# The end of a layer norm rearranged: tile 7's bias transfer ahead of tile 2's squares, tile 2 finished by VectorE in halves, one operation for the mean, epsilon on GpSimd

## The chip, the cores and the metric

One core of a Trainium2 chip runs the whole kernel. The metric is the device time in microseconds (us) of one execution; the kernel before has a median of 386.59 us over three runs (385.78 to 387.56). Engines are named as the profile names them: PE (TensorE), DVE (VectorE), ACT (ScalarE), POOL (GpSimd), SP (SyncE, which here only issues transfers).

## The reference

One decoder layer on 1024 tokens of width 1024: an input projection, three branches (spatial gating, a state-space scan, cross-attention), an output projection, and a post-norm. The change touches only the last line of it:

```
y = concatenate([y_a * silu(g_a), y_b * silu(g_b), y_x * silu(g_x)], axis=-1)
x = layer_norm(DN_ALPHA * x + y @ w_out[layer], ln_g[layer], ln_b[layer])
# layer_norm: mu = mean(x); xc = x - mu; var = mean(xc*xc)
#             xc * rsqrt(var + 1e-5) * g + b
```

## The kernel before

Tokens lie in eight tiles of 128 rows; `res[:, t]` (128x1024) holds tile t. The output projection is done in Strassen fashion, as seven products of 512-column blocks (p1 to p7), each matrix product in three passes over split operands (lines 144 to 146). The last stretch (lines 1193 to 1237) computes the last blocks tile by tile in the order of tiles 4, 5, 0, 6, 1, 7, 2, 3, and normalises a tile as soon as its last block has been added. PE, DVE, ACT and POOL execute in the order in which the code is written (`ordered("a")`, line 1043); SP's order is the scheduler's, and follows when data become ready.

For a tile t but 3 the steps are:

- `first` and `more` (DVE, lines 1094 and 1101) add a PSUM bank to `res`, and leave row sums.
- `means` (lines 1059 to 1067): two small DVE operations make minus the mean; then ACT squares the centred tile and sums it (`junk`, line 1066).
- `deviations` (1069 to 1072): DVE scales the sum and adds epsilon, POOL raises it to the power -0.5.
- `centre` (1075): DVE subtracts the mean and multiplies by gamma, in place. It therefore has to wait until ACT's squares of the same tile are done.
- `finish` (1078 to 1089): for tiles 4, 5, 6, 7 and 2 ACT multiplies by the inverse deviation (1082), a transfer issued by POOL adds the bias `lnb2` (1083), and a transfer to DRAM follows when that has landed (1084, on SP; for tile 2 on ACT's queue). For tiles 0, 1 and 3 DVE does scale and bias in one operation (1087), and the transfer goes out on SP (1089).

Tile 3 comes last. Its mean and variance come from `bn_stats` of three pieces and `bn_aggr` (1227 to 1233), epsilon is added on DVE (1234), the power is POOL's (1235), the centring DVE's (1236), and `finish(3, (0, 480, 832, 1024))` writes it out in three pieces.

Of the kernel before, what the change touches and what calls it, by code (L numbers as in the profile page):

```python
# [36 lines left out]
def trunk_kernel(ctx, tc, xT, x, w_gq, w_kv, memT, w_fm, w_v, w_o,  # L37
                 gm_wT, gm_bs, gm_g, gm_lnb, sp, b1, b2, c1, c2, dsk, glu_w, glu_b,
                 ln_gb, out):
    nc = tc.nc  # L40
# [1007 lines left out]
    stat = gm.tile([P, 64], F32, tag="nv", name="stat")  # L1048


    sums = stat[:, 0:16].rearrange("p (t c) -> p t c", c=2)
    nmean, ssq, rsd = stat[:, 16:24], stat[:, 24:32], stat[:, 32:40]
    bst = stat[:, 40:58].rearrange("p (c s) -> p c s", s=6)
    bmv = stat[:, 58:60]

    def at(t):
        return t - 4 if t >= 4 else t + 4

    def means(t0, n):
        i = slice(at(t0), at(t0) + n)  # L1060
        V.tensor_tensor(nmean[:, i], sums[:, i, 0], sums[:, i, 1], op=ALU.add)
        V.tensor_scalar(nmean[:, i], nmean[:, i], -1.0 / 1024, None, op0=ALU.mult)  # L1062
        for t in range(t0, t0 + n):
            junk = gm.tile([P, 1024], BF16, tag="mt", bufs=2, name=f"junk{t}")
            i1 = slice(at(t), at(t) + 1)
            S.activation(junk, res[:, t], AF.Square, bias=nmean[:, i1], scale=1.0,  # L1066
                         accum_out=ssq[:, i1])

    def deviations(t0, n):
        i = slice(at(t0), at(t0) + n)  # L1070
        V.tensor_scalar(rsd[:, i], ssq[:, i], 1.0 / 1024, LN_EPS, op0=ALU.mult, op1=ALU.add)  # L1071
# [2 lines left out]
    def centre(t):
        V.scalar_tensor_tensor(res[:, t], res[:, t], nmean[:, at(t):at(t) + 1], lng,
                               op0=ALU.add, op1=ALU.mult)

    def finish(t, cuts=None, queue=nc.sync):
# [237 lines left out]
```

## Time and profile before

| | us |
|---|---|
| median of three runs | 386.59 |
| the profiled execution, its own time | 383.81 |
| its span, first to last instruction | 382.1 |
| PE busy | 367.4 (96%) |
| DVE busy | 293.8 (77%) |
| ACT busy | 181.5 (48%) |
| POOL busy | 96.7 (25%) |

The span leaves 1.7 us of the profiled execution outside it. All times below are counted from the span's start. Busy shares are means over the whole program; the change lies in the last 40 us, where the profile is read instruction by instruction. A row of the timeline gives start, duration, engine, line, operation, what is written and read, and in brackets how long the engine stood idle before and what released it.

### The profile page before, as it was taken

To read this page: it belongs to the slowest core of one execution; us is meant where nothing else is said; L and a number is where in the kernel's file an instruction comes from. 1 tells how busy PE (TensorE), PEld (TensorE's weight loads), DVE (VectorE), ACT (ScalarE), POOL (GpSimd) and SP (SyncE) were. 2 spreads that over 40 slices of the span, in tenths; PEclk is the share of its full clock that TensorE was granted. 3 is DMA by queue.
4 is the path that set the end of the run, shared out by engine and by line. 5 is a ranking of instruction groups with operands and counts; after the bars stand their busy time and mean duration, and the time that the engine had idled before them with its cause. 6 is when DMAs were issued, how large, how long until landed. Compare 5 with 4: busy or idle time off the path is not lost.

```text
span 382.1 us, 5532 instructions
## 1 busy us (share of the span) xinstructions
PE 367.4 (96%) x1877; PEld 310.0 (81%) x1877; DVE 293.8 (77%) x639; ACT 181.5 (48%) x349; POOL 96.7 (25%) x87
## 2 busy tenths in 40 slices
PE   8999999999999999999999999999999999999980
PEld 7888898888888788888888888888888888877870
DVE  4699897988886599969788459775538997777783
ACT  4573597567774635232132334333424667545430
POOL 1305000001000593860873800500000022003541
PEclk9999999999999999999999999999999999999995
DMA  7984436237899776202212232400107959820988
GB/s 221 302 274 124 131 112 192 86 98 206 171 188 235 189 196 162 60 29 58 69 41 60 55 95 62 165 2 0 57 4 214 380 152 225 208 84 0 256 224 235
DMA packets 28628, 53.69 MB, mean 141 GB/s; under 512 B 5928, under 2 KB 9400, under 8 KB 27448
## 3 DMA queue, kind: packets, MB, share of 16 engines
q1 hardware_dynamic: 26296, 44.43, 38.0%
q0 software_dynamic: 2160, 8.39, 11.8%
q10 hardware_dynamic: 144, 0.52, 0.4%
q8 instruction: 15, 0.25, 0.3%
q14 instruction: 13, 0.11, 0.1%
HBM read 44.87 MB, written 13.63 MB: 153 GB/s over the span
## 4 chain that ended last, share of the span: by engine, by line
PE 67%; DVE 19%; issue 4%; ACT 4%; DMA 3%; POOL 1%; SPq 0%; POOLq 0%; DVEq 0%; ACTq 0%
PE zg L151 4%; PE zg L152 4%; PE zg L154 4%; PE zv L144 3%; PE zv L146 3%; PE zv L145 3%; PE av L624 2%; PE zxb L152 2%; PE zxb L154 2%; PE zxb L151 2%; PE q L152 2%; PE q L154 2%; PE q L151 2%; DVE l_u L62 2%; DMA r_wo<-in_w_o_dram 2%
## 5 line engine op out<-in xcount | busy, mean ns | idle before, releaser
L144 PE MATMUL zv<-h_v,xh 128*128 128x512 f32 x64 | 25.6, 400 | 0.3 <-ACT yb L229 0.3
L151 PE MATMUL zu<-xh,h_u 128*128 128x512 f32 x64 | 25.9, 404 | 0.0
L151 PE MATMUL zg<-xh,h_g 128*128 128x512 f32 x64 | 25.5, 398 | 0.0
L152 PE MATMUL zu<-xl,h_u 128*128 128x512 f32 x64 | 25.0, 391 | 0.0
L152 PE MATMUL zg<-xl,h_g 128*128 128x512 f32 x64 | 25.0, 390 | 0.0
L146 PE MATMUL zv<-h_v,xl 128*128 128x512 f32 x64 | 25.0, 390 | 0.0
L145 PE MATMUL zv<-l_v,xh 128*128 128x512 f32 x64 | 24.9, 389 | 0.0
L1029 POOL DMA_DIRECT2D l_wo<-ws_s x6 | 5.2, 863 | 72.8 <-ACT l_wo L1028 66.0
L65 ACT CAST h_v<-r_v 128x512 fp32r<-128x512 f32 x16 | 9.9, 619 | 26.5 <-PE zu L152 18.6
L62 DVE TENSOR_TENSOR l_v<-r_v,h_v 128x512 fp32r<-128x512 f32 x16 | 16.7, 1050 | 6.3 <-ACT h_v L65 6.2
L154 PE MATMUL zu<-xh,l_u 128*128 128x512 f32 x64 | 19.8, 390 | 0.0
L154 PE MATMUL zg<-xh,l_g 128*128 128x512 f32 x64 | 19.7, 390 | 0.0
L596 ACT ACTIVATE pr<-s,nm 128x256 f32<-128x256 f32 x32 | 14.9, 473 | 7.9 <-DVE nm L592 6.5
L1072 POOL TENSOR_TENSOR stat<-stat,nhalf 128x1 f32<-128x1 f32 x7 | 10.3, 1466 | 24.1 <-DVE stat L1071 24.1
L1066 ACT ACTIVATE junk<-res,stat 128x1024 bf16<-128x1024 f32 x7 | 8.1, 1150 | 16.6 <-DVE stat L1062 15.2
L902 DVE TENSOR_SCALAR nv<-nv,mv,rsv 128x128 f32<-128x128 f32 x32 | 13.3, 487 | 3.0 <-POOL rsv L896 3.0
L144 PEld LDWEIGHTS zv<-h_v,xh 128*128 128x128 f32 x64 | 12.0, 188 | 3.0 <-ACT yb L229 0.7
L62 DVE TENSOR_TENSOR l_wo<-r_wo,h_wo 128x512 fp32r<-128x512 f32 x18 | 12.1, 686 | 2.7 <-ACT h_wo L65 2.7
L154 PEld LDWEIGHTS zu<-xh,l_u 128*128 128x128 f32 x64 | 12.0, 188 | 2.6
L146 PEld LDWEIGHTS zv<-h_v,xl 128*128 128x128 f32 x64 | 12.0, 188 | 2.6
L154 PEld LDWEIGHTS zg<-xh,l_g 128*128 128x128 f32 x64 | 12.0, 188 | 2.6
L151 PEld LDWEIGHTS zg<-xh,h_g 128*128 128x128 f32 x64 | 12.0, 188 | 2.3
(371 smaller groups left out, 1187.2 us busy)
## 6 DMA issues: line engine op xcount, KB each, us to landing
r_v<-in_w_v_dram SPq DMA_DIRECT2D x16, 256.0 KB, 2.9
ws_s<-in_w_o_dram SPq DMA_DIRECT2D x4, 1024.0 KB, 6.2
r_wo<-ws_s SPq DMA_DIRECT2D x16, 256.0 KB, 3.4
res<-in_x_dram SPq DMA_DIRECT2D x4, 1024.0 KB, 11.7
r_x<-in_xT_dram SPq DMA_DIRECT2D x15, 256.0 KB, 4.5
r_wo<-in_w_o_dram SPq DMA_DIRECT2D x12, 256.0 KB, 4.4
out_dram<-res SPq DMA_DIRECT2D x6, 512.0 KB, 4.0
res<-lnp POOLq DMA_DIRECT2D x5, 512.0 KB, 4.6
```

Of the source, the lines that this page charges most:

```text
L62: eng.tensor_tensor(o, a, b, op=ALU.subtract)
L65: S.copy(hi, src)
L144: T.matmul(ps, lhsT=sh, rhs=mh, start=start, stop=False, **kw)
L145: T.matmul(ps, lhsT=sh, rhs=ml, start=False, stop=False, **kw)
L146: T.matmul(ps, lhsT=sl, rhs=mh, start=False, stop=stop, **kw)
L151: T.matmul(ps[h], lhsT=wh, rhs=xh[:, kt, half[h]], start=first, stop=False, **kw[h])
L152: T.matmul(ps[h], lhsT=wh, rhs=xl[:, kt, half[h]], start=False, stop=False, **kw[h])
L154: T.matmul(ps[h], lhsT=wl, rhs=xh[:, kt, half[h]], start=False, stop=last, **kw[h])
L596: S.activation(pr[:, h], ps3[:, h], AF.Exp, bias=nm[:, h:h + 1], scale=1.0, accum_out=rs[:, h:h + 1])
L902: V.tensor_scalar(sl, sl, mv[:, i, 0:1], rs[:, i:i + 1], op0=ALU.subtract, op1=ALU.mult)
L1066: S.activation(junk, res[:, t], AF.Square, bias=nmean[:, i1], scale=1.0, accum_out=ssq[:, i1])
L1072: G.tensor_tensor(rsd[:, i], rsd[:, i], nhalf[:, 0:n], op=ALU.pow)
```

## The change

The mean of a tile is made in one DVE operation, `(sum0 + sum1) * fracs`, which gives -1/1024 and -1/32768 of the sum in two columns; the second is the bias of ACT's squares, whose scale is now 1/32, so that their sum is the variance itself. Epsilon is added on POOL, just ahead of the power, for all eight tiles (`inverse`). `finish(7)` moves from after tile 2's squares to before them. Tile 2 is centred into another buffer (`cent2`), straight after its mean; it is finished by DVE in two halves, one between tile 3's last two pieces and one after tile 3's centring, each with its own transfer on SP. Of tile 3's three output transfers the middle one goes to ACT's queue.

```
-    def means(t0, n):
-        V.tensor_tensor(nmean[:, i], sums[:, i, 0], sums[:, i, 1], op=ALU.add)
-        V.tensor_scalar(nmean[:, i], nmean[:, i], -1.0 / 1024, None, op0=ALU.mult)
-            S.activation(junk, res[:, t], AF.Square, bias=nmean[:, i1], scale=1.0,
-                         accum_out=ssq[:, i1])
-    def deviations(t0, n):
-        V.tensor_scalar(rsd[:, i], ssq[:, i], 1.0 / 1024, LN_EPS, op0=ALU.mult, op1=ALU.add)
-        G.tensor_tensor(rsd[:, i], rsd[:, i], nhalf[:, 0:n], op=ALU.pow)
+    def mean(t):
+        V.scalar_tensor_tensor(nmean[:, i], sums[:, i, 0:1].to_broadcast([P, 2]), sums[:, i, 1:2],
+                               fracs, op0=ALU.add, op1=ALU.mult)
+    def square(t):
+        S.activation(junk, res[:, t], AF.Square, bias=nmean[:, i, 1:2], scale=1.0 / 32,
+                     accum_out=ssq[:, i:i + 1])
+    def inverse(t, var):
+        G.tensor_scalar(rsd[:, i], var, LN_EPS, None, op0=ALU.add)
+        G.tensor_tensor(rsd[:, i], rsd[:, i], nhalf[:, 0:1], op=ALU.pow)
+    def centre(t, dst=None):
+        V.scalar_tensor_tensor(res[:, t] if dst is None else dst, res[:, t],
+                               nmean[:, at(t), 0:1], lng, op0=ALU.add, op1=ALU.mult)
+    def finish(t, cuts=None, src=None, queues=(nc.sync,)):
...
+        for i, (a, b) in enumerate(zip(cuts, cuts[1:])):
+            V.scalar_tensor_tensor(ot[:, a:b], src[:, a:b], rs, lnb2[:, a:b], op0=ALU.mult,
                                    op1=ALU.add)
-            nc.sync.dma_start(out=out[tok[t], a:b], in_=ot[:, a:b])
+            queues[i % len(queues)].dma_start(out=out[tok[t], a:b], in_=ot[:, a:b])
...
         first(j, 1, ub[j], -1, True)
+        deviation(5 + j)
+        centre(5 + j)
+        if j == 2:
+            finish(7)
...
-        else:
-            finish(7)
+    deviation(2)
+    centre(2, cent2)
     p4(3)
-    deviations(2, 1)
-    centre(2)
-    finish(2, None, nc.scalar)
     first(3, 1, ub[3], -1)
...
         V.bn_stats(bst[:, 1 + c], res[:, 3, cols[0]:cols[1]])
+        if c == 0:
+            finish(2, (0, 512), cent2)
     V.bn_aggr(bmv, bst.rearrange("p c s -> p (c s)"))
-    V.tensor_scalar(rsd[:, at(3):at(3) + 1], bmv[:, 1:2], LN_EPS, None, op0=ALU.add)
-    G.tensor_tensor(rsd[:, at(3):at(3) + 1], rsd[:, at(3):at(3) + 1], nhalf[:, 0:1], op=ALU.pow)
+    inverse(3, bmv[:, 1:2])
     V.scalar_tensor_tensor(res[:, 3], res[:, 3], bmv[:, 0:1], lng, op0=ALU.subtract, op1=ALU.mult)
-    finish(3, (0, 480, 832, 1024))
+    finish(2, (512, 1024), cent2)
+    finish(3, (0, 480, 832, 1024), queues=(nc.sync, nc.scalar))
```

How instructions stand on DVE from tile 2's last addition to tile 3's centring, before; `o_3568` and `o_3569` are the PSUM banks of tiles 2 and 3, `o2last` the bank of tile 3's last 256 columns:

```order
L1101 SCALAR_TENSOR_TENSOR res,stat<-o_3568,res 128x512
L1061 TENSOR_TENSOR stat<-stat 128x1
L1062 TENSOR_SCALAR stat<-stat 128x1
L1071 TENSOR_SCALAR stat<-stat 128x1
L1075 SCALAR_TENSOR_TENSOR res<-res,stat,lnp 128x1024
L1094 SCALAR_TENSOR_TENSOR res<-res,o_3128 128x512
L1227 BN_STATS stat<-res 128x6
L1101 SCALAR_TENSOR_TENSOR res<-o_3569,res 128x256
L1232 BN_STATS stat<-res 128x6
L1101 SCALAR_TENSOR_TENSOR res<-o2last,res 128x256
L1232 BN_STATS stat<-res 128x6
L1233 BN_AGGR stat<-stat 128x2
```

The same stretch of DVE now, with `cent2` a part of `stat`:

```order
L1115 SCALAR_TENSOR_TENSOR res,stat<-o_3571,res 128x512
L1066 SCALAR_TENSOR_TENSOR stat<-stat,fracs 128x2
L1088 SCALAR_TENSOR_TENSOR stat<-res,stat,lnp 128x1024
L1108 SCALAR_TENSOR_TENSOR res<-res,o_3131 128x512
L1239 BN_STATS stat<-res 128x6
L1115 SCALAR_TENSOR_TENSOR res<-o_3572,res 128x256
L1244 BN_STATS stat<-res 128x6
L1101 SCALAR_TENSOR_TENSOR res<-stat,lnp 128x512
L1115 SCALAR_TENSOR_TENSOR res<-o2last,res 128x256
L1244 BN_STATS stat<-res 128x6
L1247 BN_AGGR stat<-stat 128x2
L1249 SCALAR_TENSOR_TENSOR res<-res,stat,lnp 128x1024
```

Tile 2's centring stands where it stood but reads nothing that ACT's squares make, one 128x512 operation of tile 2 (line 1101) has come in ahead of tile 3's last addition, and the small operations on the mean and epsilon are one instead of three.

ACT's last instructions before: `junk_3720` are the squares of tile 7, `junk_3761` those of tile 2, and the `res<-res,stat` rows scale tiles 6, 7 and 2:

```order
L1066 ACTIVATE junk_3720,stat<-res,stat 128x1024
L1082 ACTIVATE res<-res,stat 128x1024
L1066 ACTIVATE junk_3761,stat<-res,stat 128x1024
L1082 ACTIVATE res<-res,stat 128x1024 x2
L1084 DMA out_dram<-res 128x1024
```

And now, where `junk_3717` are the squares of tile 7 and `junk_3760` those of tile 2:

```order
L1072 ACTIVATE junk_3701,stat<-res,stat 128x1024
L1072 ACTIVATE junk_3717,stat<-res,stat 128x1024
L1095 ACTIVATE res<-res,stat 128x1024 x2
L1072 ACTIVATE junk_3760,stat<-res,stat 128x1024
L1103 DMA out_dram<-res 128x352
```

Tile 7's scaling now stands ahead of tile 2's squares, which wait behind it; tile 2's scaling is gone.

POOL's last instructions before, from tile 6's bias transfer on:

```order
L1083 DMA res<-lnp 128x1024
L1072 TENSOR_TENSOR stat<-stat,nhalf 128x1
L1083 DMA res<-lnp 128x1024
L1072 TENSOR_TENSOR stat<-stat,nhalf 128x1
L1083 DMA res<-lnp 128x1024
L1235 TENSOR_TENSOR stat<-stat,nhalf 128x1
```

And now:

```order
L1096 DMA res<-lnp 128x1024
L1081 TENSOR_SCALAR stat<-stat 128x1
L1082 TENSOR_TENSOR stat<-stat,nhalf 128x1
L1096 DMA res<-lnp 128x1024
L1081 TENSOR_SCALAR stat<-stat 128x1
L1082 TENSOR_TENSOR stat<-stat,nhalf 128x1
L1081 TENSOR_SCALAR stat<-stat 128x1
L1082 TENSOR_TENSOR stat<-stat,nhalf 128x1
```

Tile 2's bias transfer, which stood ahead of tile 3's power, is gone; each power has an addition ahead of it.

## Rows read from the trace of the kernel before

**Rows 1.** Windows: busy us (instructions) by engine, clock, DMA share, GB/s.

```profile
345.00:362.50 17.50, 17.46 (x75) 14.15 (x76) 13.55 (x35) 8.62 (x13) 8.66 (x7) 1.00 0.49 128
362.50:371.00 8.50, 8.45 (x49) 7.17 (x47) 6.96 (x14) 3.13 (x5) 4.04 (x4) 1.00 0.79 239
375.20:382.10 6.90, 0.00 (x0) 0.00 (x0) 0.76 (x2) 0.00 (x0) 0.00 (x0) 0.50 0.76 257
```

**Rows 2.** Timeline of DVE: tiles 7, 1, 2 and 3, start and duration in us.

```profile
363.24 1.27 DVE L1075 SCALAR_TENSOR_TENSOR res<-res,stat,lnp 128x1024 f32<-128x1024 f32 x1
364.43 1.28 DVE L1087 SCALAR_TENSOR_TENSOR res<-res,stat,lnp 128x1024 f32<-128x1024 f32 x1
...
368.15 1.27 DVE L1075 SCALAR_TENSOR_TENSOR res<-res,stat,lnp 128x1024 f32<-128x1024 f32 x1
369.34 0.68 DVE L1094 SCALAR_TENSOR_TENSOR res<-res,o 128x512 f32<-128x512 f32 x1
...
371.45 0.41 DVE L1101 SCALAR_TENSOR_TENSOR res<-o2last,res 128x256 f32<-128x256 f32 x1
...
372.69 1.27 DVE L1236 SCALAR_TENSOR_TENSOR res<-res,stat,lnp 128x1024 f32<-128x1024 f32 x1
374.42 1.54 DVE L1087 SCALAR_TENSOR_TENSOR res<-res,stat,lnp 128x480 f32<-128x480 f32 x3 [0.46 <-POOL stat L1235]
```

**Rows 3.** Timeline of POOL, the same stretch.

```profile
364.13 1.97 POOL L1072 TENSOR_TENSOR stat<-stat,nhalf 128x1 f32<-128x1 f32 x1
369.38 0.87 POOL L1083 DMA_DIRECT2D res<-lnp  x1 [3.28 <-ACT res L1082]
369.99 0.85 POOL L1072 TENSOR_TENSOR stat<-stat,nhalf 128x1 f32<-128x1 f32 x1
...
372.93 1.45 POOL L1235 TENSOR_TENSOR stat<-stat,nhalf 128x1 f32<-128x1 f32 x1
```

**Rows 4.** Issues of transfers: line, count, KB, us from issue to landing.

```profile
out_dram<-res SPq DMA_DIRECT2D x1, 512.0 KB, 2.6
res<-lnp POOLq DMA_DIRECT2D x1, 512.0 KB, 4.5
out_dram<-res SPq DMA_DIRECT2D x1, 96.0 KB, 4.2
```

**Rows 5.** Line 1089, SP's issues: durations in ns, first and last start.

```profile
L1089 SPq DMA_DIRECT2D out_dram<-res x5: 332/842/1217, 357.8 to 376.9; - x5
```

**Rows 6.** Timeline of DVE, ACT and PE around the last weight's split.

```profile
342.12 0.16 DVE L1061 TENSOR_TENSOR stat<-stat 128x1 f32<-128x1 f32 x1
342.32 0.15 DVE L1062 TENSOR_SCALAR stat<-stat 128x1 f32<-128x1 f32 x1
...
343.65 0.60 ACT L65 CAST h_wo<-r_wo 128x512 fp32r<-128x512 f32 x1
...
345.04 0.50 PE L145 MATMUL o<-l_wo,T4h 128*128 128x512 f32 x1 [0.22 <-DVE l_wo L62]
```

**Rows 7.** Timeline of PE: the last matmul of tile 3's two stages.

```profile
367.71 0.39 PE L146 MATMUL o<-h_wo,T4l 128*128 128x512 f32 x1
...
370.67 0.28 PE L146 MATMUL o2last<-yx_wo,B21l 128*128 128x256 f32 x1
```

**Rows 8.** Timeline of ACT: tile 2's squares, then tile 7's scaling.

```profile
366.80 1.15 ACT L1066 ACTIVATE junk<-res,stat 128x1024 bf16<-128x1024 f32 x1 [3.57 <-DVE stat L1062]
...
367.95 1.14 ACT L1082 ACTIVATE res<-res,stat 128x1024 f32<-128x1024 f32 x1
```

**Rows 9.** Timeline of DVE and POOL in the middle of the program.

```profile
129.62 0.69 DVE L56 TENSOR_TENSOR L<-Fr,B 128x512 f32<-128x512 f32 x1 [2.15 <-DMA ws_s<-ot]
...
133.29 1.53 POOL L56 TENSOR_TENSOR S<-sn,cn 128x512 f32<-128x512 f32 x1
133.92 1.46 DVE L56 TENSOR_TENSOR t<-Fi,B 128x512 f32<-128x512 f32 x1
```

**Rows 10.** Timeline of POOL: a small constant written, line 799.

```profile
180.86 0.10 POOL L799 MEMSET H<- 128x4 f32 x1 [12.01 <-DVE t L793]
```

More of the change, by code (lines that the diff above doesn't have):

```diff
@@ L251, in trunk_kernel @@
     G.memset(nhalf, -0.5)
+    fracs = const.tile([P, 2], F32, name="fracs")
+    G.memset(fracs[:, 0:1], -1.0 / 1024)
+    G.memset(fracs[:, 1:2], -1.0 / 32768)
     kh = kvq.tile([P, 4, 256], F32R, name="kh")
@@ L1047, in trunk_kernel @@
     lng, lnb2 = lnp[:, 0], lnp[:, 1]
-    stat = gm.tile([P, 64], F32, tag="nv", name="stat")
+    stat = gm.tile([P, 1092], F32, tag="nv", name="stat")
     sums = stat[:, 0:16].rearrange("p (t c) -> p t c", c=2)
-    nmean, ssq, rsd = stat[:, 16:24], stat[:, 24:32], stat[:, 32:40]
-    bst = stat[:, 40:58].rearrange("p (c s) -> p c s", s=6)
-    bmv = stat[:, 58:60]
+    nmean = stat[:, 16:32].rearrange("p (t c) -> p t c", c=2)
+    ssq, rsd = stat[:, 32:40], stat[:, 40:48]
+    bst = stat[:, 48:66].rearrange("p (c s) -> p c s", s=6)
@@ L1056, in at @@
+    bmv = stat[:, 66:68]
+    cent2 = stat[:, 68:1092]
     def at(t):
         return t - 4 if t >= 4 else t + 4
-    def means(t0, n):
-        i = slice(at(t0), at(t0) + n)
-        V.tensor_tensor(nmean[:, i], sums[:, i, 0], sums[:, i, 1], op=ALU.add)
-        V.tensor_scalar(nmean[:, i], nmean[:, i], -1.0 / 1024, None, op0=ALU.mult)
-        for t in range(t0, t0 + n):
-            junk = gm.tile([P, 1024], BF16, tag="mt", bufs=2, name=f"junk{t}")
-            i1 = slice(at(t), at(t) + 1)
-            S.activation(junk, res[:, t], AF.Square, bias=nmean[:, i1], scale=1.0,
-                         accum_out=ssq[:, i1])
@@ L1069, in deviations @@
-    def deviations(t0, n):
-        i = slice(at(t0), at(t0) + n)
-        V.tensor_scalar(rsd[:, i], ssq[:, i], 1.0 / 1024, LN_EPS, op0=ALU.mult, op1=ALU.add)
-        G.tensor_tensor(rsd[:, i], rsd[:, i], nhalf[:, 0:n], op=ALU.pow)
[L1074 to L1078, printed above, removed]
+    def mean(t):
+        i = at(t)
+        V.scalar_tensor_tensor(nmean[:, i], sums[:, i, 0:1].to_broadcast([P, 2]), sums[:, i, 1:2],
+                               fracs, op0=ALU.add, op1=ALU.mult)
@@ new lines, in square, with means @@
+    def square(t):
+        junk = gm.tile([P, 1024], BF16, tag="mt", bufs=2, name=f"junk{t}")
+        i = at(t)
+        S.activation(junk, res[:, t], AF.Square, bias=nmean[:, i, 1:2], scale=1.0 / 32,
+                     accum_out=ssq[:, i:i + 1])
+    def means(t):
+        mean(t)
+        square(t)
+    def inverse(t, var):
+        i = slice(at(t), at(t) + 1)
+        G.tensor_scalar(rsd[:, i], var, LN_EPS, None, op0=ALU.add)
+        G.tensor_tensor(rsd[:, i], rsd[:, i], nhalf[:, 0:1], op=ALU.pow)
@@ L1079, in finish, with deviation @@
+    def deviation(t):
+        inverse(t, ssq[:, at(t):at(t) + 1])
+    def centre(t, dst=None):
+        V.scalar_tensor_tensor(res[:, t] if dst is None else dst, res[:, t],
+                               nmean[:, at(t), 0:1], lng, op0=ALU.add, op1=ALU.mult)
+    def finish(t, cuts=None, src=None, queues=(nc.sync,)):
         rs = rsd[:, at(t):at(t) + 1]
@@ L1083, in finish @@
             G.dma_start(out=ot, in_=lnb2, accum_op=ALU.add)
-            queue.dma_start(out=out[tok[t]], in_=ot)
+            nc.sync.dma_start(out=out[tok[t]], in_=ot)
             return
-        for a, b in zip(cuts, cuts[1:]):
-            V.scalar_tensor_tensor(ot[:, a:b], ot[:, a:b], rs, lnb2[:, a:b], op0=ALU.mult,
+        src = ot if src is None else src
+        for i, (a, b) in enumerate(zip(cuts, cuts[1:])):
+            V.scalar_tensor_tensor(ot[:, a:b], src[:, a:b], rs, lnb2[:, a:b], op0=ALU.mult,
                                    op1=ALU.add)
-            nc.sync.dma_start(out=out[tok[t], a:b], in_=ot[:, a:b])
+            queues[i % len(queues)].dma_start(out=out[tok[t], a:b], in_=ot[:, a:b])
     def first(t, c, ps, sign, total=False):
@@ L1178, in p7_done @@
         more(4 + j, 1, ub[j], -1, True)
-        means(4 + j, 1)
+        means(4 + j)
     def p4(j):
@@ L1190, in p2_done @@
         more(j, 0, z2[j], 1, True)
-        means(j, 1)
+        means(j)
     p7(0)
@@ L1197, in trunk_kernel @@
     p7_done(1)
-    deviations(4, 1)
+    deviation(4)
     centre(4)
@@ L1216, in trunk_kernel @@
             p7_done(j + 2)
-            deviations(j, 1)
+            deviation(j)
             centre(j)
             finish(5 + j)
-        else:
-            finish(7)
+    deviation(2)
+    centre(2, cent2)
     p4(3)
-    deviations(2, 1)
-    centre(2)
-    finish(2, None, nc.scalar)
     first(3, 1, ub[3], -1)
```

4 lines of the change are left out of this document (removed).

## The prediction
> **What bounds the kernel now.** I read the windows first. From 345.0 to 371.0 us PE has no idle time worth naming (17.46 of 17.50 us busy, then 8.45 of 8.50), and from 375.2 to the span's end at 382.1 no engine but DVE does anything, for 0.76 us, while the transfers move 257 GB/s, 1.8 MB in all [rows 1]. So the end has three parts: PE until its last matmul ends at 370.67 + 0.28 = 370.95 [rows 7]; then a chain over DVE, ACT and POOL; then the draining of the output.
>
> The timelines of the three engines show the chain. ACT squares tile 2 at 366.80 and scales tile 7 only at 367.95 [rows 8]. DVE centres tile 2 in place at 368.15, after those squares, so it starts tile 3's first addition at 369.34, though PE had ended that product at 367.71 + 0.39 = 368.10 [rows 2, 7]. It reaches tile 3's last addition at 371.45, 0.50 after PE's end, and centres tile 3 at 372.69 to 373.96. The finish of tile 3 waits 0.46 for POOL's power, which runs from 372.93 to 374.38, and starts at 374.42 [rows 2, 3]. Its third transfer is issued at 376.9 and takes 4.2 to land, at 381.1; the span ends 1.0 later [rows 4, 5]. An output tile of 512 KB that left at 368.12 took 2.6 [rows 4]: the 4.2 us for 96 KB is a queue of other outputs, tile 7's and tile 2's among them, which both had to wait for a bias transfer of 4.5 us.
>
> **A trait of POOL that the sum needs.** The power takes 0.85 us at 369.99, while DVE works with one operand from PSUM. At 372.93 it takes 1.45 and ends 0.42 after DVE's centring of tile 3; at 364.13 it takes 1.97 and ends 0.39 after the second of two DVE operations that overlap it, 364.43 + 1.28 = 365.71 [rows 2, 3]. Those DVE operations read two operands from SBUF, and POOL waits for their end. From 0.85 and 0.40 I estimate that a power asks for its operand about 0.45 after its start. POOL gets in between two such DVE operations if it is waiting when the first ends: in the middle of the program both engines alternate, each 128x512 operation taking about 1.5 us where DVE's takes 0.69 alone [rows 9]. At 364.13 the power would have asked at 364.58, after the second had begun.
>
> **The change, part by part**, in the times of this execution.
>
> *Mean in one operation.* Tile 4's mean stands on PE's path: mean, squares on ACT, then ACT's cast of the last weight at 343.65, its split on DVE, and PE, which waits for it at 345.04 [rows 6]. One of two dependent operations goes, 342.32 - 342.12 = 0.20. Ends: 0, if the two-column form is slower by as much, and 0.22, the wait that the row gives PE. I take 0.2, and all PE work after it comes 0.2 sooner. The other means lie beside PE; on DVE they and epsilon free some 0.2 us a tile, which I don't count.
>
> *Tile 2 centred elsewhere.* Centring follows the mean, at about 366.4, and is over by 367.7. Tile 3's first addition then starts when PE lets it, at 368.10 - 0.2 = 367.9, 1.4 sooner. From there to the last addition it was 371.45 - 369.34 = 2.11; tile 2's first half adds about 0.68 (the duration of a 128x512 operation), so DVE is ready at 370.7. PE's product ends at 370.95 - 0.2 = 370.75, and the addition follows at 370.8: 0.65 sooner than 371.45. The new half costs nothing as long as DVE's wait for PE hides it; that cover is 0.1 us thin, and beyond it each microsecond costs one.
>
> *Tile 7's transfer sooner.* Its power is held, as now, until DVE's finish of tile 1 ends. The addition of epsilon ahead of it falls into tile 7's centring and gets in between the two DVE operations, so the power still ends near 366.0. ACT scales tile 7 at 366.05 to 367.2, POOL issues the bias at 367.5 instead of 369.38, it lands at 372.0, and tile 7 goes out 1.9 sooner. What is pushed back: tile 2's squares wait behind the scaling, 367.2 instead of 366.80, until 368.4. On POOL epsilon and the power of tile 2 follow. No row shows the addition of one column; the ends are 0.10, a small constant written [rows 10], and 0.85, a power. I take 0.25, nearer to the first since there is no power in it. Then tile 2's deviation is there at 368.5 + 0.25 + 0.85 = 369.6 (370.2 at the upper end), and DVE wants it at 370.1. It just fits.
>
> *Epsilon on POOL, tile 3.* Centring now starts at 372.69 - 0.65 = 372.04 and ends at 373.3. The addition waits on POOL for it, is over at 373.6, and the power takes 0.85 after it, 374.45; DVE meanwhile does tile 2's second half (0.68, to 374.0). Finish of tile 3: 374.5, as late as before (374.42). The lower end is 374.05, if POOL's addition gets in ahead of the centring; the upper 375.3, if it has to wait out tile 2's half as well (374.0 + 0.4 + 0.85). So all that DVE gained up to here is spent by the second half and by epsilon.
>
> In a sentence of its own: the Trainium skill, SBUF — State Buffer, section Who interferes with whom, says that a VectorE instruction with two SBUF inputs contends with a GpSimd instruction that reads SBUF, and that the one issued second is blocked until the other ends, and by that rule alone the two additional GpSimd reads of tile 3 speak against moving epsilon; the rows above agree on the blocking with 0.39 to 0.42 us.
>
> *The output.* DVE's last piece ends 1.54 after the finish's start [rows 2], at 376.0. The third transfer was issued at 376.9, SP's issues taking up to 1.2 us [rows 5]. With the second on ACT's queue it goes between 376.05 and 376.4; I take 376.2, 0.7 sooner. Tile 2's bias transfer is gone from the end, and its 512 KB of output no longer wait for it: its halves leave at 370.8 and 374.0, tile 7 at 372.0. Left for the end is tile 3 alone, 512 KB in three pieces within a microsecond. Landing: 2.6 us at most by the lone tile of 512 KB, less 416 KB at some 0.4 MB per us, 1.6, at least; 4.2 if nothing eases. I take 2.2, 2.0 less than now.
>
> **Sum:** 0.7 (issue) + 2.0 (landing) = 2.7 us off 381.1, the span's last 1.0 unchanged. The profiled execution would go from 383.81 to 381.1. The median of the timed runs lies 2.78 above it, and I take the gain off that: 386.59 - 2.7 = 383.9.
>
> **The rivals.**
>
> *POOL stays shut out.* If POOL doesn't get in between two DVE operations, epsilon of tile 7 is over at 365.9, its power asks at 366.3, just as tile 2's centring begins, and ends at 368.0. Scaling to 369.1, tile 2's squares to 370.3, its deviation at 371.5, 1.4 after DVE wanted it, and DVE stands still. Tile 3's finish starts near 376.3, the third transfer goes at 378.1, and the gain is 381.1 - 380.3 = 0.8: 385.8. For it: the power at 364.13 lay across two operations. Against it: the alternation.
>
> *The last transfer takes 4 us anyway.* Then only the issue counts, 0.7: 385.9. For it: the 4.2 of only 96 KB. Against it: the 2.6, which is of the same kind and five times the size.
>
> *The deviation on DVE's path, slower than before.* One mechanism: tile 2's first half stands in DVE's order ahead of tile 3's last addition and waits for POOL; if the addition of epsilon costs as much as a power (0.85) and is shut out each time, tile 3's finish starts at 377.3 or later. It decides from 374.42 + 2.7 = 377.1 on, where the gain at the end is used up. With the third transfer at 379.0 and a landing of 2.6 to 4.2 the span is 0.5 to 2.1 longer; 387.9 at the middle. For it: DVE executes in order, and the cover is thin. Against it: an addition has no power in it.
>
> **How the numbers follow.** Chances: forecast 0.63, its own range 382.9 to 385.0 (from 374.05 and a landing of 1.6, to 375.3 and one of 2.6); POOL shut out 0.17; landing unchanged 0.12; slower 0.08. About 0.5%, 1.9 us, is what a measurement can tell from no change. Of the forecast 0.85 lies beyond it, 0.53, and almost nothing of the two middle cases; slower than 0.5% is half of the last case, and a little for what I have not seen, 0.06. Same takes the other 0.40. The range goes from 382.6 to 386.3, which takes in both middle cases and leaves out the slower one.
>
> **What would show it.** Right: PE's last matmul ends near 370.75; tile 7's bias is issued near 367.5; DVE's last addition to tile 3 follows PE within 0.1; tile 3's finish starts between 374.0 and 375.3, released by POOL; the last landing takes about 2 us. Wrong: DVE idle before tile 2's first half with POOL as releaser; the power of tile 7 ending 0.4 after tile 2's centring; landings still near 4 us.

## The result: 380.57 us in the first timing, and what the profile after shows

The changed kernel took 380.57 us (median of four executions: 378.28, 378.81, 382.34, 383.14) against 386.18 before, ratio 0.9851 [0.9818, 0.9885]. That is 5.6 us where 2.7 were forecast, and outside the range. Timed twice more against the kernel before it gave 382.49 (ratio 0.992 [0.9888, 0.9951]) and 381.75 (0.9893 [0.9844, 0.9942]). The median of its 16 executions (378.28 to 383.85) is 382.4, that of 61 of the kernel before (382.27 to 387.80) 385.9: 3.5 us. One more execution of the kernel before, of 1346 us, is left out of this.

The profiled execution is the one of 382.34 us, with a span of 380.6. The end is read relative to PE's last matmul, which I call P: P = 370.95 before and 372.18 + 0.28 = 372.46 after. From P to the span's end it was 11.14 us and is now 8.16: 2.98 less, more than the profiled execution gained altogether (1.5). PE itself ends 1.5 later than before: 2.4 were lost near 130 us, and 0.8 came back in other stretches. That is the subject of the section after next.

DVE behind P, of the kernel after, answering [rows 2]:

```profile
371.86 0.73 DVE L1101 SCALAR_TENSOR_TENSOR res<-stat,lnp 128x512 f32<-128x512 f32 x1
372.52 0.42 DVE L1115 SCALAR_TENSOR_TENSOR res<-o2last,res 128x256 f32<-128x256 f32 x1
...
373.70 1.29 DVE L1249 SCALAR_TENSOR_TENSOR res<-res,stat,lnp 128x1024 f32<-128x1024 f32 x1
374.90 0.75 DVE L1101 SCALAR_TENSOR_TENSOR res<-stat,lnp 128x512 f32<-128x512 f32 x1
376.11 1.54 DVE L1101 SCALAR_TENSOR_TENSOR res<-res,stat,lnp 128x480 f32<-128x480 f32 x3 [0.46 <-POOL stat L1082]
```

The last addition to tile 3 follows PE by 0.06, and the finish starts at P + 3.65, later than before (374.42 - 370.95 = 3.47). So DVE's chain behind PE has not become shorter at all. POOL from tile 6's bias transfer on, answering [rows 3]:

```profile
364.86 0.94 POOL L1096 DMA_DIRECT2D res<-lnp  x1 [2.99 <-ACT res L1095]
365.51 1.68 POOL L1081 TENSOR_SCALAR stat<-stat 128x1 f32<-128x1 f32 x1
367.27 0.57 POOL L1082 TENSOR_TENSOR stat<-stat,nhalf 128x1 f32<-128x1 f32 x1
369.32 0.92 POOL L1096 DMA_DIRECT2D res<-lnp  x1 [1.49 <-ACT res L1095]
370.25 0.29 POOL L1081 TENSOR_SCALAR stat<-stat 128x1 f32<-128x1 f32 x1
370.62 0.58 POOL L1082 TENSOR_TENSOR stat<-stat,nhalf 128x1 f32<-128x1 f32 x1
373.75 1.31 POOL L1081 TENSOR_SCALAR stat<-stat 128x1 f32<-128x1 f32 x1 [2.55 <-DVE stat L1247]
375.15 0.92 POOL L1082 TENSOR_TENSOR stat<-stat,nhalf 128x1 f32<-128x1 f32 x1
```

Tile 7's bias is issued at P - 3.14 instead of P - 1.57. The issues at the end, answering [rows 4] (where the last number is missing, the landing could not be told apart):

```profile
res<-lnp POOLq DMA_DIRECT2D x1, 512.0 KB, 5.1
out_dram<-res SPq DMA_DIRECT2D x2, 256.0 KB, 3.7
out_dram<-res SPq DMA_DIRECT2D x1, 240.0 KB, 2.0
out_dram<-res ACTq DMA_DIRECT2D x1, 176.0 KB, 2.1
out_dram<-res SPq DMA_DIRECT2D x1, 96.0 KB
```

The third transfer of tile 3 is issued at P + 5.21 (before P + 5.95), and from there to the span's end it is 2.95 us instead of 5.19. Its landing was not recorded; if the span's last 1.0 us is as before, it came near 379.6, about 1.9 us after the issue. What matters more is how busy the DMA engines are. Windows behind P of the kernel before, in the columns of [rows 1]:

```profile
370.95:373.00 2.05, 0.00 (x0) 0.00 (x0) 1.91 (x7) 1.07 (x1) 0.68 (x2) 1.00 1.02 194
373.00:375.00 2.00, 0.00 (x0) 0.00 (x0) 1.54 (x2) 0.00 (x0) 1.39 (x2) 0.72 0.86 164
375.00:377.00 2.00, 0.00 (x0) 0.00 (x0) 0.96 (x3) 0.00 (x0) 0.00 (x0) 0.50 1.03 260
377.00:379.00 2.00, 0.00 (x0) 0.00 (x0) 0.00 (x0) 0.00 (x0) 0.00 (x0) 0.50 1.04 394
379.00:381.10 2.10, 0.00 (x0) 0.00 (x0) 0.00 (x0) 0.00 (x0) 0.00 (x0) 0.50 0.68 251
381.10:382.10 1.00, 0.00 (x0) 0.00 (x0) 0.00 (x0) 0.00 (x0) 0.00 (x0) 0.50 0.00 0
```

And of the kernel after:

```profile
372.47:374.50 2.03, 0.00 (x0) 0.00 (x0) 1.93 (x5) 0.00 (x0) 0.75 (x1) 1.00 1.00 299
374.50:376.50 2.00, 0.00 (x0) 0.00 (x0) 1.54 (x3) 0.00 (x0) 1.49 (x2) 1.00 1.03 406
376.50:378.50 2.00, 0.00 (x0) 0.00 (x0) 1.15 (x3) 0.00 (x0) 0.00 (x0) 0.62 0.84 319
378.50:379.60 1.10, 0.00 (x0) 0.00 (x0) 0.00 (x0) 0.00 (x0) 0.00 (x0) 0.50 0.58 202
379.60:380.63 1.03, 0.00 (x0) 0.00 (x0) 0.00 (x0) 0.00 (x0) 0.00 (x0) 0.50 0.00 0
```

The column before the last is the share of the 16 DMA engines. Length times share, summed, is 2.09 + 1.72 + 2.06 + 2.08 + 1.43 = 9.38 us of all engines before, and 2.03 + 2.06 + 1.68 + 0.64 = 6.41 after: 2.97 less, beside the 2.98 that the end became shorter. Before, that is 9.38 us of work in the 10.15 us up to 381.10.

That the two differences agree so closely is partly chance. In the second profile of the changed kernel (P = 371.70) the tail is 8.17, but the engines have only 1.96 + 1.32 + 1.98 + 0.68 = 5.94 us of work in it, and stand idle for 0.7 us of the second window:

```profile
371.70:373.70 2.00, 0.00 (x0) 0.00 (x0) 1.90 (x5) 0.00 (x0) 0.71 (x1) 1.00 0.98 199
373.70:375.70 2.00, 0.00 (x0) 0.00 (x0) 1.54 (x3) 0.00 (x0) 1.52 (x2) 0.87 0.66 258
375.70:377.70 2.00, 0.00 (x0) 0.00 (x0) 1.19 (x3) 0.00 (x0) 0.00 (x0) 0.50 0.99 378
377.70:378.90 1.20, 0.00 (x0) 0.00 (x0) 0.00 (x0) 0.00 (x0) 0.00 (x0) 0.50 0.57 196
```

So the engines' load accounts for the end before the change, and not by itself for the end after it.

While a bias transfer runs alone, the engines are full (1.02) at 194 GB/s; with outputs alone they pass 394 and 406. At 200 GB/s the 512 KB of tile 2's bias are 2.6 us of all engines, which I put down as an estimate from these windows; a run below takes the transfer away.

### The profile page after: what moved, and what is told of

It reads as the page before. It is cut to its first block, busy times and chain, and to the rows that moved or that the text cites. A ratio compares the mean times of both kernels' runs of the same rounds, so it can differ in the third digit from the quotient of the medians.

```text
span 380.6 us, 5529 instructions
## 1 busy us (share of the span) xinstructions
PE 367.3 (96%) x1877; PEld 309.8 (81%) x1877; DVE 293.1 (77%) x626; ACT 180.5 (47%) x348; POOL 96.6 (25%) x96
## 4 chain that ended last, share of the span: by engine, by line
PE 74%; DVE 15%; issue 3%; DMA 3%; ACT 2%; POOL 1%; SPq 0%; POOLq 0%; DVEq 0%; ACTq 0%
PE o L145 4%; PE zg L151 4%; PE zg L152 4%; PE zg L154 4%; PE o L146 4%; PE o L144 4%; PE zv L144 3%; PE zv L146 3%; PE zv L145 3%; PE av L627 2%; PE zxb L152 2%; PE zxb L151 2%; PE zxb L154 2%; PE q L152 2%; PE q L154 2%
## 5 line engine op out<-in xcount | busy, mean ns | idle before, releaser
L62 DVE TENSOR_TENSOR l_v<-r_v,h_v 128x512 fp32r<-128x512 f32 x16 | 15.7, 986 | 6.1 <-ACT h_v L65 6.1
L152 PEld LDWEIGHTS zg<-xl,h_g 128*128 128x128 f32 x64 | 12.0, 188 | 2.3
```

The source lines that it names most:

```text
L62: eng.tensor_tensor(o, a, b, op=ALU.subtract)
L152: T.matmul(ps[h], lhsT=wh, rhs=xl[:, kt, half[h]], start=False, stop=False, **kw[h])
```

## The experiments: where the end's gain comes from

"Tail" is the time from P to the span's end in the profiled execution. In the unchanged kernels it is 11.14 and 11.17 before, and 8.16, 8.17 and 8.21 after, so that tenths count even in a single profile. The variants were profiled once each.

**The change without one of its parts** (each the changed kernel with one part undone; the changed kernel's tail is 8.16). Theory P is the prediction's chain.

Epsilon on DVE again:

```
-        G.tensor_scalar(rsd[:, i], var, LN_EPS, None, op0=ALU.add)
+        V.tensor_scalar(rsd[:, i], var, LN_EPS, None, op0=ALU.add)
```

> The changed kernel with epsilon added by DVE again, in one operation ahead of each power, all else as changed. Read is the tail, span less PE's last end: 11.1 before, 8.2 in the changed kernel. Theory P (the prediction's chain): POOL's addition for tile 3 waits out the centring and its power waits out tile 2's second half; with the addition on DVE the power alone gets in when the centring ends, tile 3's finish follows tile 2's second half at once, and the tail is 7.8, 0.3 to 0.4 shorter. Theory Q (queue): the tail is the draining of the output alone, and the tail stays at 8.2 within 0.1.

Tail 8.65: both missed. Tile 2's epsilon on DVE waits for ACT's squares, and what is written behind it, tile 2's centring, waits with it:

```profile
368.64 0.15 DVE L1081 TENSOR_SCALAR stat<-stat 128x1 f32<-128x1 f32 x1 [1.37 <-ACT junk L1072]
368.72 1.28 DVE L1088 SCALAR_TENSOR_TENSOR stat<-res,stat,lnp 128x1024 f32<-128x1024 f32 x1
...
375.78 1.54 DVE L1101 SCALAR_TENSOR_TENSOR res<-res,stat,lnp 128x480 f32<-128x480 f32 x3
```

Tile 3's finish starts at P + 4.08 (P = 371.70), its third transfer is issued 0.44 later than in the changed kernel, and the end comes 0.49 later. So epsilon on POOL is what lets centring into another buffer be early; its price on POOL (1.31 at 373.75) is real and is less than this.

Tile 7's bias transfer behind tile 2's squares again:

```
-        if j == 2:
-            finish(7)
...
+    finish(7)
     deviation(2)
```

> The changed kernel with tile 7's scaling and bias transfer after tile 2's squares, as before. By P tile 7's bias is issued 1.2 later, its output leaves 1.2 later beside tile 3's pieces, and tile 2's power on POOL stands behind the issue, so that DVE waits about 0.2 for it ahead of tile 2's first half: tail 8.4 to 9.2. By Q, with 512 KB more in the last stretch, 9.2 or more.

Tail 9.31, just above P's span and in Q's. Tile 2's power comes behind the later issue, and DVE waits in front of tile 2's first half, the "wrong" sign of the prediction and P's mechanism, at 0.64 instead of 0.2:

```profile
373.53 0.75 DVE L1101 SCALAR_TENSOR_TENSOR res<-stat,lnp 128x512 f32<-128x512 f32 x1 [0.64 <-POOL stat L1082]
```

Tile 3's finish starts 0.74 later for it, and tile 7's bias and output fall later as well; the run does not divide the 1.15 between the two.

Tile 2 finished by ACT and a bias transfer again, everything else as changed:

```
+    S.activation(res[:, 2], cent2, AF.Copy, scale=rsd[:, at(2):at(2) + 1])
+    G.dma_start(out=res[:, 2], in_=lnb2, accum_op=ALU.add)
+    nc.scalar.dma_start(out=out[tok[2]], in_=res[:, 2])
...
-        if c == 0:
-            finish(2, (0, 512), cent2)
...
-    finish(2, (512, 1024), cent2)
```

> The changed kernel with tile 2 finished as before, by ACT's scaling, POOL's bias transfer and an output on ACT's queue, but still centred into the other buffer, so that DVE does not wait for the squares. By P DVE's finish of tile 3 starts 0.4 earlier than in the changed kernel, with no half of tile 2 in between, but tile 2's output leaves only when the bias has landed, near 377 on the scale of the changed profile, and lands 2.6 to 4 later: tail 8.5 to 9.8. By Q the tail is back near 11.

Tail 10.28, between the two: with the bias transfer in place, the rest of the change is worth 0.9. Tile 7's bias is issued at P - 3.14 here, as in the changed kernel, and not at P - 1.57, and more of the engines' work is done ahead of P. The 3 us ahead of P of the kernel before, then of this one:

```profile
367.95:370.95 3.00, 3.00 (x25) 2.79 (x23) 2.84 (x5) 1.21 (x3) 1.46 (x2) 1.00 0.84 315
368.03:371.03 3.00, 3.00 (x25) 2.79 (x23) 2.23 (x4) 1.85 (x3) 1.66 (x3) 1.00 1.05 347
```

That is 0.6 us of the 0.9.

Tile 2 centred in place:

```
-    centre(2, cent2)
+    centre(2)
...
-            finish(2, (0, 512), cent2)
+            finish(2, (0, 512))
...
-    finish(2, (512, 1024), cent2)
+    finish(2, (512, 1024))
```

> The changed kernel with tile 2 centred in place, so that DVE waits for ACT's squares, and finished by DVE in halves as changed. By P tile 3's first addition starts 1.8 later than in the changed kernel, the whole chain behind it is DVE's, and the tail is 9.6 to 9.9. By Q, since the output to be drained is the same, it stays below 8.7.

Tail 9.81, as P said, and Q fell: centring waits 2.20 for the squares, and everything behind it is late by 1.65.

**The third transfer on SP.**

```
-    finish(3, (0, 480, 832, 1024), queues=(nc.sync, nc.scalar))
+    finish(3, (0, 480, 832, 1024), queues=(nc.sync,))
```

> The changed kernel with all three transfers of tile 3 on SP. Theory A, the prediction's (ACT's queue spares the third transfer SP's long issue): SP's second issue lasts 1.1 us as before, the third goes 0.6 to 0.75 later, tail 8.7 to 8.9. Rival Q (the long issue came from outputs that stood in the queue, which are gone now): SP's issues take 0.33, the third goes at 5.2 to 5.3 after PE's last matmul as it does now, tail 8.1 to 8.3.

Tail 8.18: theory A fell. SP's issues of 1.1 us are gone although ACT's queue is not used, as rival Q had it; the third is issued at P + 5.32 instead of 5.21. The second queue is worth 0.11 at the issue and 0.02 at the end.

**Only tile 2's bias transfer taken out of the kernel before.** No other part of the change is in it.

```
-            G.dma_start(out=ot, in_=lnb2, accum_op=ALU.add)
+            if t != 2:
+                G.dma_start(out=ot, in_=lnb2, accum_op=ALU.add)
```

> The kernel before without tile 2's bias transfer (tile 2 goes out without its bias), everything else as it was: centring in place, the same order, the same queues. Theory D (the end is bound by the 16 DMA engines: a bias transfer of 512 KB holds all of them for 2.6 us at 200 GB/s, outputs pass at 390 GB/s): tail 8.1 to 8.9 instead of 11.17, a gain of 2.3 to 3.0. Rival C (the gain of the change at the end comes from DVE's earlier chain and the second queue): tail 10.4 or more.

Tail 8.20, with DVE's chain as it was (finish of tile 3 at P + 3.45). Its issues and windows behind P:

```profile
out_dram<-res SPq DMA_DIRECT2D x1, 96.0 KB, 2.1
```

```profile
373.75:375.75 2.00, 0.00 (x1) 0.00 (x0) 1.86 (x7) 1.10 (x1) 0.09 (x1) 1.00 1.05 199
375.75:377.75 2.00, 0.00 (x0) 0.00 (x0) 1.56 (x2) 0.00 (x0) 1.42 (x1) 0.54 0.93 328
377.75:379.75 2.00, 0.00 (x0) 0.00 (x0) 1.00 (x3) 0.00 (x0) 0.00 (x0) 0.50 1.00 389
379.75:380.95 1.20, 0.00 (x0) 0.00 (x0) 0.00 (x0) 0.00 (x0) 0.00 (x0) 0.50 0.51 175
```

The landing of the 96 KB falls from 4.2 to 2.1 and its issue comes 0.83 sooner, by this one transfer alone; SP's issues last 0.33 to 0.40 here too. The engines have work for 2.10 + 1.86 + 2.00 + 0.61 = 6.57 us behind P, 2.81 less than before, and the tail is 2.94 less. With the transfer goes the wait of tile 2's output for it (issued at P + 1.13 instead of P + 5.94), but the engines had only 0.8 us to spare in the 10.15, so that wait can account for no more than that. Theory C fell. Taking away the 512 KB that the DMA engines add up is enough for the whole gain at the end; the earlier transfer of tile 7, which belongs to the 0.9 while tile 2's transfer is there, adds nothing to it. The other parts of the change see to it that DVE can do that work without making the end later.

**Does the load of the DMA engines still set the end?** Three kernels on the changed one with a small copy (next section, called free). "best" puts epsilon of tile 3 alone back on DVE:

```
-    inverse(3, bmv[:, 1:2])
+    i3 = slice(at(3), at(3) + 1)
+    V.tensor_scalar(rsd[:, i3], bmv[:, 1:2], LN_EPS, None, op0=ALU.add)
+    G.tensor_tensor(rsd[:, i3], rsd[:, i3], nhalf[:, 0:1], op=ALU.pow)
```

> The changed kernel with the gate's transfer reading a small copy, and epsilon of tile 3 alone back on DVE, ahead of its centring. Theory E (the end is a chain of sums: POOL's addition held until the centring's end, then the power of 0.9): the power now starts with the centring, ends 0.4 after it, and DVE finishes tile 3 straight after tile 2's half, at 3.3 to 3.35 us after PE's last matmul instead of 3.64. Tail (PE's last matmul to the span's end) 7.8 to 7.9 instead of 8.16, time 0.3 below that of free_after, 380.5 to 380.7, ratio to before 0.986 to 0.989. Rival B (epsilon on DVE costs what it did for all eight tiles): the power is held through tile 2's half as well, finish at 3.9 or later, tail 8.4 to 8.7.

DVE did what E said, with no wait for POOL left:

```profile
371.63 1.27 DVE L1253 SCALAR_TENSOR_TENSOR res<-res,stat,lnp 128x1024 f32<-128x1024 f32 x1
372.82 0.74 DVE L1103 SCALAR_TENSOR_TENSOR res<-stat,lnp 128x512 f32<-128x512 f32 x1
373.49 1.53 DVE L1103 SCALAR_TENSOR_TENSOR res<-res,stat,lnp 128x480 f32<-128x480 f32 x3
```

The finish starts at P + 3.17 and the third transfer goes 0.49 sooner, but the tail is 8.14: landings became longer by as much (240 KB 2.4, 176 KB 2.5 instead of 2.0 and 2.1). 381.22 us (ratio 0.9875 [0.9842, 0.9907]), no better than free. Both theories missed the tail. So a shorter chain alone gains nothing, while a later one costs at once (0.44 and 0.49 with epsilon on DVE): in the changed kernel the chain and the transfers bind within a few tenths of each other. In this profile the engines stand still for 0.64 us between P + 2 and P + 4 (share 0.68), and tile 7's output leaves at P + 2.38, when its bias has landed; from then on 1280 KB of output are issued.

Without tile 7's bias transfer as well:

```
-            G.dma_start(out=ot, in_=lnb2, accum_op=ALU.add)
+            if t != 7:
+                G.dma_start(out=ot, in_=lnb2, accum_op=ALU.add)
```

> The version called best without tile 7's bias transfer (tile 7 goes out without its bias). Theory D: the DMA engines have 2.6 us less to do around PE's end, the third transfer of tile 3 finds them free and lands in 1.6 to 1.9 instead of 2.4, tail 7.3 to 7.6 instead of 8.14. Rival F (a landing of that size is what such a transfer takes, whatever else moves): 8.1.

Tail 7.72, 0.42 less, on D's side and 0.1 short of its span. The engines now stand still ahead of tile 3's pieces, so here the chain binds, and with this chain 0.42 is all that is left to take from the engines' load:

```profile
372.07:374.07 2.00, 0.00 (x0) 0.00 (x0) 2.00 (x4) 0.00 (x0) 0.99 (x1) 0.61 0.00 0
374.07:376.07 2.00, 0.00 (x0) 0.00 (x0) 0.70 (x2) 0.00 (x0) 0.00 (x0) 0.50 0.97 358
```

Epsilon of tile 7 on DVE too, so that its bias transfer is issued sooner:

```
-        G.tensor_scalar(rsd[:, i], var, LN_EPS, None, op0=ALU.add)
+        (V if t == 7 else G).tensor_scalar(rsd[:, i], var, LN_EPS, None, op0=ALU.add)
```

> The version called best with epsilon of tile 7 on DVE as well, so that its power waits for the end of its own centring alone and its scaling and bias transfer come 1.4 us sooner. Theory D: the engines' gap ahead of tile 7's output (0.5 to 0.7 us within the 3 us after PE's last matmul) closes, tail 7.5 to 7.8 instead of 8.14, and the time is 0.3 to 0.6 below that of best, ratio to before 0.984 to 0.988. Rival F: tail 8.1, no difference from best.

Tail 8.18 and 381.76 us (0.9876 [0.9831, 0.9921]): the expectation drawn from D missed, and F's 8.1 came out. The bias is issued 1.4 sooner (P - 4.56) and lands 7.0 later instead of 5.5:

```profile
res<-lnp POOLq DMA_DIRECT2D x1, 512.0 KB, 7.0
```

Tile 7's output leaves at P + 2.41 as in best (2.38). The engines are full for the 6 us ahead of P (shares of 0.91 to 1.08 in each), first with tile 6's bias and tile 1's output, so that an earlier issue only waits longer: the same theory, which I had not applied to the time ahead of P.

## The experiments: where the other two microseconds come from

The starts of PE's matmuls 720, 760, 1740 and 1760, counted from 0, divide each profiled execution (us):

| kernel | to 720 | to 760 | to 1740 | to 1760 | to P | tail | span |
|---|---|---|---|---|---|---|---|
| before | 131.92 | 7.77 | 200.65 | 5.95 | 24.65 | 11.14 | 382.1 |
| before, again | 132.08 | 8.63 | 200.62 | 5.88 | 24.65 | 11.17 | 383.0 |
| before, mean in one operation | 132.54 | 12.00 | 199.09 | 6.48 | 24.75 | 10.87 | 385.7 |
| before, free | 132.46 | 7.70 | 200.63 | 6.04 | 24.65 | 11.17 | 382.7 |
| after | 131.49 | 10.15 | 200.56 | 5.54 | 24.74 | 8.16 | 380.6 |
| after, again | 131.63 | 9.29 | 200.56 | 5.52 | 24.70 | 8.17 | 379.9 |
| after, a third time | 131.91 | 7.79 | 200.63 | 5.70 | 24.70 | 8.21 | 378.9 |
| after, free | 131.73 | 7.70 | 200.98 | 5.65 | 24.74 | 8.16 | 379.0 |

The column "to 760" swings by up to 4 us. Its cause is a transfer of 32 bytes on SP's queue, for which DVE (and POOL) wait at about 129 to 133 us. In the kernel after the wait was 4.53, where it was 2.15 before [rows 9], and in the kernel before with the one-operation mean 4.80:

```profile
131.57 0.69 DVE L56 TENSOR_TENSOR L<-Fr,B 128x512 f32<-128x512 f32 x1 [4.53 <-DMA ws_s<-ot]
```

```profile
132.89 0.69 DVE L56 TENSOR_TENSOR L<-Fr,B 128x512 f32<-128x512 f32 x1 [4.80 <-DMA ws_s<-ot]
```

Up to about 2.2 us the wait costs PE next to nothing, and beyond that about what it grows by, but for the longest: waits of 2.15, 2.19, 3.03, 3.73, 4.53 and 4.80 (before; after, a third time; before, again; after, again; after; the one-operation mean) go with 7.77, 7.79, 8.63, 9.29, 10.15 and 12.00 in the column, and no wait with 7.70. Of the 12.00, 1.5 come back by matmul 1740.

DVE waits only because the transfer reads the tile `ot`, whose memory the next step wants. "Free" copies the 8 columns first, so that the transfer holds nothing that is wanted:

```
-            last_ot.append(ot[0:1, 0:8])
+            gt = const.tile([P, 8], F32, tag="gt", bufs=8, name=f"gt{lq}{hp}")
+            V.tensor_copy(gt, ot[:, 0:8])
+            last_ot.append(gt[0:1, :])
```

The kernels unchanged, and both with this copy, on one chip:

> The kernel before, unchanged, timed again. Theory E (the end): the change gains some 3 us after PE's last matmul and 0.3 ahead of it; the rest of the measured 5.6 us is an earlier stretch that varies from execution to execution, above all the landing of a 32-byte transfer near 126 us on which DVE and POOL wait (2.9 us in the profile of before, 5.3 in that of after). By E the single times of this kernel spread over 3 us or more, span less PE's last end is again 11.1, and the ratio to the kernel before is 1.000 within 0.004. Theory U (upstream): the change itself shortens a stretch before 345 us by some 2.5 us, by moved buffers or two operations more at the start; then this kernel's times lie close together, 385 to 387.

> The changed kernel, unchanged, timed again. By E its median lies 3 to 4 us below that of before once both are timed often (ratio 0.990 to 0.992), its single times fall in two or more levels up to 4 us apart, and the levels differ by the wait on the 32-byte transfer; span less PE's last end is 8.2 again. By U the ratio is 0.985 again, and PE's last end lies 2.5 us below that of before in profiles with the same wait on that transfer.

> The kernel before, with the eight floats that the 32-byte transfer reads copied by DVE into a small tile of their own, so that the memory of the attention buffers can be reused without waiting for its landing. By E the wait of DVE and POOL near 129 us goes (2.2 and 2.8 us in the profile), the time falls by 2 to 4 us against before, and the spread of the single times shrinks. By U the same, since U says nothing of it; the two differ in the next kernel.

> The changed kernel with the same copy. By E the difference to the kernel before with the copy is 3.3 us within 0.7, since what varies is gone from both, and the levels of the single times draw together. By U the difference is 5 to 6 us as in the first timing.

Unchanged: 385.7 (ratio of before to itself 0.9992 [0.997, 1.0013]) and 382.49 (0.992). With the copy: 383.65 (0.9944 [0.992, 0.9969]) and 380.93 (0.9886 [0.9854, 0.9919]). The wait is gone, DVE goes on at once,

```profile
127.17 0.17 DVE L640 COPY gt<-ot 128x8 f32<-128x8 f32 x1
127.44 0.69 DVE L56 TENSOR_TENSOR L<-Fr,B 128x512 f32<-128x512 f32 x1
```

and 2.05 us are gained by it in the kernel before, 1.56 in the changed one. Between the two the difference is then 383.65 - 380.93 = 2.7, unchanged 385.7 - 382.49 = 3.2; both lie in E's spans, and U's 5 to 6 us did not come again. Three details of E missed: the single times of the kernel before spread over 2.6 us and not 3, those of the changed kernel (381.58 to 383.35) fall into no levels, and the spread did not shrink with the copy (3.0 before, 2.1 after, against 2.6 and 1.8 unchanged). So other stretches vary as well. The changed kernel with the copy is the fastest of these four.

The changed kernel a third time, to see whether the first timing's level belongs to it:

> The changed kernel, unchanged, once more against the kernel before. Theory E (the change is worth 3.0 us behind PE's last matmul and 0.4 ahead of it): ratio 0.989 to 0.993, tail 8.16; where executions lie near 378.5 again, the profile or the spread shows it in the stretch around 126 to 140 us, not in the last 40. Rival L (the level of 378 us belongs to the change): ratio 0.984 to 0.987.

381.75, ratio 0.9893, at the edge of E's span; its interval [0.9844, 0.9942] takes in L's span too. One of the six executions took 378.65, like two of the first four; none of the low ones was the profiled one, so what they did otherwise stays open. The 32-byte transfer alone does not explain them: the profiled execution here took 380.64 with a column "to 760" of 7.79, near the least that any has, and with the copy none of six took less than 380.52, while one with the copy and epsilon of tile 7 on DVE took 378.86. Apart from the first timing the twelve executions have a median of 382.5, 3.4 below the 385.9 of the kernel before.

The one-operation mean alone:

> The kernel before with the mean in one DVE operation and the squares scaled by 1/32, nothing else (epsilon stays on DVE, where it multiplies by 1). Theory E: PE's wait for the last weight's split shrinks, so that the 20 matmuls around 340 to 347 us take 5.75 to 5.85 us instead of 5.9 to 6.0; tail 11.1 to 11.2 as before. Rival M (the one operation makes all of the 0.4): 5.5 to 5.6.

6.48 between matmuls 1740 and 1760: both missed. The kernel itself took 387.43, in a single execution. PE waits twice in this stretch. The wait for the last weight's split, on which the prediction's 0.2 stood, is 0.17 instead of 0.22 [rows 6] (0.16 in the kernel after). The other, 1.10 here and 0.18 in the kernel after, is for an addition that DVE does late:

```profile
346.06 0.50 PE L144 MATMUL o<-h_wo,T4h 128*128 128x512 f32 x1 [1.10 <-DVE res L1105]
348.83 0.51 PE L145 MATMUL o<-l_wo,T4h 128*128 128x512 f32 x1 [0.17 <-DVE l_wo L62]
```

So the term is 0.05. (The tail of this kernel is 10.87; POOL's power for tile 7 took 0.93 there instead of 1.97 [rows 3].) Why that column is 5.5 to 5.7 in all four profiles of the table with the change and 5.9 to 6.5 in those without it is not settled; among the changed kernel's variants it went from 5.11 to 6.18. That it is DVE's backlog from earlier is a guess from the wait of 1.10.

## Why the prediction was wrong

**The step that failed** is the last of the sum: "386.59 - 2.7 = 383.9". It put everything ahead of the end but the mean's 0.2 at nothing, took the median of three executions as a fixed base, and let the range follow from bounds of the end alone. But executions of one kernel differ by 5 us, in stretches that the change does not touch, and a median of four against one of four carries that. Of the measured 5.6, 2.98 are at the end, about 0.4 lie between matmuls 1740 and 1760 (cause open), and the other 2.2 are the level of the first four executions, which two further timings did not repeat. What made those four fast stays open. Against 3.4 the forecast is short by 0.7, and 382.5 would still be 0.1 below the range. The prediction itself had 1.9 us as what a measurement can tell, and went only 0.3 below its own lower end of 382.9 with the range. The wait of 2.15 on a 32-byte transfer stood in [rows 9], read only for how DVE and POOL alternate; but its swing could not be read off one profile, in which it cost PE 0.07. More timings of the kernel before would have shown a spread.

**The end's terms** came out near their sizes, the first of them by luck. Issue: 0.7 forecast, 0.74 measured. Landing: 2.0 forecast, 2.24 by the time from the issue to the span's end. Both come from tile 2's bias transfer, as the kernel before without it shows (0.83 and 2.1). For the landing the prediction had named that transfer among the reasons; the 0.7 it gave to ACT's queue, which gives 0.11 at the issue and 0.02 at the end. By the Trainium skill, DMA: Bandwidth & Descriptors, section Issuing engines are not separate DMA queues, transfers from SP, ACT and POOL run on the same 16 engines, and several issuers save only issuing time; the 0.02 agrees. I had written that the 4.2 is "a queue of other outputs"; the engines' time under a transfer that adds I had not taken from the windows, although 375.20 to 382.10 stood there with a share of 0.76 [rows 1], its last 1.0 us empty.

**What bounds the kernel** was therefore read wrongly. I described the end as a chain over DVE, ACT and POOL and then the draining. That "all that DVE gained up to here is spent" was right (finish at P + 3.65, forecast 374.5 - 370.75 = 3.75), but before the change this chain carried no weight: it is the same without tile 2's bias transfer (P + 3.45), and the end is 2.94 sooner. In the changed kernel it binds on one side: 0.48 sooner in best changed the end by 0.02, 0.44 and 1.65 later made it 0.49 and 1.65 later.

**POOL between two DVE operations.** Half right. For tile 3 the addition got in at the centring's end (374.99), 0.07 behind it, as forecast, and the power ended 0.42 behind tile 2's half. For tile 7 it did not: the addition shows from 365.51 on, ahead of the centring's end at 365.92, and yet took 1.68, to 367.19, 0.07 after tile 1's finish. The issue of tile 6's bias ran until 365.80, just ahead of that finish (365.84), which is a likely reason and was not tested. The power then ran unhindered, in 0.57 instead of the 0.85 that I used, so that scaling still came at P - 4.60 (forecast 366.05 - 370.75 = -4.70) and the bias at P - 3.14 (forecast -3.25). It landed 5.1 later, not 4.5. The addition's 0.25 was 0.22 to 0.29. The 0.85 was misread in one point: at 369.99 DVE was mostly at the statistics of tile 3 (370.05), with one operand from SBUF, and not at an addition from PSUM.

**The mean** was worth 0.05, not 0.2: of the two operations' 0.35 the wider one needs 0.22, and PE's wait fell by less still.

**The rivals.** "The last transfer takes 4 us anyway" fell at 1.9. "POOL stays shut out" was true of the addition for tile 7, without its price, since a power that nobody hinders is 0.28 cheaper; its own sum was also 0.4 too long, since 1.4 us of waiting put tile 3's finish near 375.9, not 376.3. "The deviation on DVE's path" did not come about: DVE's wait before tile 2's first half is nil, and it appears, with 0.64, when tile 7's transfer is put back.

## What to carry to other kernels

Where the last microseconds are transfers, sum length times DMA share over the windows behind the last matmul before following the chain. If the share is near 1, as before the change, less work for the DMA engines makes the end shorter (2.94 here). An earlier issue helps only as far as it moves work into time in which the engines are free (part of 0.9 here, and nothing where they were full), and a second queue did not help. A bias added by a transfer costs the engines about twice what an output of the same size does; next to the end VectorE did it at no cost that the end shows (tail 8.16, against 8.20 where nobody adds it). Then look again: once the load is down, the chain can be the bound. And before a gain of 1% is taken off a median, time the kernel often enough to see how far its executions differ, look for a wait that does, and put the swing into the range.

## What the runs showed of the hardware that I had not expected

- A transfer that adds into SBUF holds all 16 engines (shares 1.02 and 1.05) at 194 and 199 GB/s; outputs to DRAM pass at 389 to 406. By the Trainium skill, Collectives: The Full Stack, section The bandwidth ceiling: the fold count and why AG ≠ RS ≠ AR, a ReduceScatter runs at half the rate of an AllGather, because its add needs two source reads. That is said of collectives between cores; for this transfer within one core the factor of two agrees, and no run here shows the reason.
- Two of SP's last three issues took 1.14 and 0.84 us in the kernel before, and all three 0.33 to 0.41 in both kernels without tile 2's bias transfer that use SP alone for tile 3. What in the queues makes an issue long is not shown.
- POOL's power of one column takes 0.57 after an addition, 0.85 to 0.93 directly after a transfer's issue, and a one-column addition 0.22 to 0.29. Beside DVE operations with two operands from SBUF an addition took 1.31 and 1.68 and ended 0.07 after them; a power ended 0.39 to 0.42 after.
- A transfer of 32 bytes made DVE wait up to 4.80 us, since it held memory that the next step wanted; a copy of 0.17 us removes that.
